# A two-layer hybrid trunk on one core: stationary weight tiles set off by 128 or 192 bytes instead of 64

## The chip, the core and the metric

The kernel runs on one core of one Trainium2 chip. The metric is the device time of one execution in microseconds (us), the median over several runs. Below, TensorE is PE and its separate row for weight loads is PEld; VectorE is DVE, ScalarE is ACT, GpSimd is POOL, and SP is the engine that issues nearly all DMAs.

## What is computed

A sequence of 256 tokens of width 2048 goes through two layers. Each layer is a token mixer and an MLP, each behind an RMSNorm whose scale and shift come from a condition vector `c`:

```python
for i in range(DEPTH):                      # DEPTH = 2
    sh1, sc1, g1, sh2, sc2, g2 = split(silu(c) @ ada_w[i] + ada_b[i])
    h = modulate(rmsnorm(x, norm_mix[i]), sh1, sc1)
    y = attn_pool_mixer(h, ...) if i % 2 == 0 else ssd_mixer(h, ...)
    x = x + g1 * y
    h = modulate(rmsnorm(x, norm_ffn[i]), sh2, sc2)
    x = x + g2 * (square(relu(h @ ffn_w1[i])) @ ffn_w2[i])   # 2048 -> 8192 -> 2048
return rmsnorm(x, final_norm)
```

Everything is float32. Layer 0 mixes by dilated window attention and pooling, layer 1 by a Mamba-2 style SSD scan. Nearly all the arithmetic is in the projections: each weight is read from HBM once, 661 MB in all with the conditioning weights.

## The kernel before

**Products in three parts.** A float32 operand is split into `hi`, its value rounded to the format of the fast matmul (float32r), and `lo`, the rest. A product is three matmuls: hi by hi, hi by lo and lo by hi. The activations `h` lie turned, with the contraction on the partitions, as tiles of 256 columns of `hi` followed by 256 columns of `lo` (`Hidden.tile`, aligned to 256 bytes).

**Two ways to multiply.** Where the weights are the stationary operand (`gemm_ws` and `up_wide`, through `mm` with `one=True`, L198 to L200), each matmul loads a 128 by 128 block of weights and streams 256 columns of activations past it; every one of the three has its own weight load. The three write one accumulator of 256 columns. Where the activations are the stationary operand (`gemm_xs`, through `xs_step`, L274 to L276), 512 columns of weights stream past.

**Who uses which.** The first projection of an MLP (`up`) has the weights stationary, the second (`down`) the activations. In the first MLP a wide sweep (`up_wide`) does the first quarter of `up` row by row with eight accumulators; in the second MLP the first block goes through `opening`, whose matmuls are 512 and 256 columns in turn (L245, L246). After that an MLP alternates: four `down` blocks of 192 matmuls of 512 columns, then three or four `up` blocks of 192 matmuls of 256 columns. The attention mixer uses `gemm_ws` for q, k and the pooling input, between the heads' small matmuls; the SSD mixer uses it for the conv inputs, two blocks of three accumulators for each of eight groups (the first of all goes through `opening`). The part of q that rides along in the attention mixer's first sweep (`half_row`) goes through the same `mm`.

**Where the weights lie.** A weight chunk of 1 MB comes in by one DMA into `raw`; `split` (L162) makes `hi` on ACT (L166) and `lo` on DVE (L167), in two halves. `hi` and `lo` are tiles of a pool with four buffers each, whose start is a multiple of `ALIGN` = 256 bytes, and the data begin `off` elements behind the start. `gemm_ws` with `one=True` and `load_row` pass `off` = `SHIFT` = 16 elements, which is 64 bytes; `gemm_xs`, `opening` and `half_row` pass nothing, so their data begin on the multiple of 256 bytes. A block of 128 columns is 512 bytes on a partition, so every stationary block of `gemm_ws` starts 64 bytes past a multiple of 256.

**What sets the order.** The code is written in the order in which each engine runs it; semaphores are set by the framework from the tiles. PE has no work of its own to choose from. Conditioning tiles (`ada_run`, L86) are fed in between by a counter (`Feed`).

Of the kernel before, what the change touches and what calls it, by code (L numbers as in the profile page):

```python
# [9 lines left out]
F32R = mybir.dt.float32r  # L10
# [5 lines left out]
P = 128  # L16
T = 256
D = 2048
# [2 lines left out]
GROUPS = 8  # L21
WINDOWS = (2, 4, 8, 16)

ALIGN, SHIFT = 256, 16


C_NMIX, C_NFFN, C_FIN, C_ADAB = 0, 32, 64, 80
# [11 lines left out]
def trunk(ctx, tc, xin, cb, fin, adaT, par, m0, m1, tri_in, icnt, pw_in,  # L39
# [5 lines left out]
    wp = ctx.enter_context(tc.tile_pool(name="weights", bufs=4))  # L45
# [3 lines left out]
    misc = ctx.enter_context(tc.tile_pool(name="miscp", bufs=3, space=PSUM))  # L49
    dram = ctx.enter_context(tc.tile_pool(name="scratch", bufs=1, space=DRAM))  # L50


    ones = const.tile([P, P], F32, name="ones")
    V.memset(ones, 1.0)
# [45 lines left out]
    def ada_jobs(l, kinds, n=4):  # L100
        jobs = []
        for k0 in range(0, KT, n):
            for kt in range(k0, k0 + n):
                for i in kinds:
                    jobs.append((l, i, kt, n if kt == k0 + n - 1 else 0))
        return jobs
# [47 lines left out]
    def load(ap, nk, width, off=0):  # L154

        raw = wp.tile([P, D], F32, name="raw")
        SP.dma_start(raw[:, 0:nk * width], ap)
        half = nk // 2
        parts = [split(wp, raw[:, s * half * width:(s + 1) * half * width], half, off) for s in range(2)]
        feed[0].tick()  # L160
        return parts

    def split(pool, src, rows, off=0):
        n = src.shape[1]
        hi, lo = (pool.tile([P, D // 2 + SHIFT], F32R, name=name, align_bytes=ALIGN)[:, off:off + n] for name in ("hi", "lo"))
        S.activation(hi, src, AF.Copy)  # L166
        V.tensor_tensor(lo, src, hi.bitcast(F32), op=ALU.subtract)  # L167
        return hi.rearrange("p (k w) -> p k w", k=rows), lo.rearrange("p (k w) -> p k w", k=rows), rows

    class Stream:  # L170
# [5 lines left out]
        def half(self, i):  # L176
            while len(self.halves) <= i:
                n = len(self.halves)
                ap, nk = self.aps[n // 2]
                if n % 2 == 0:  # L180
                    self.raw = wp.tile([P, D], F32, name="raw")
                    SP.dma_start(self.raw[:, 0:nk * self.width], ap)
                size = nk // 2 * self.width
                self.halves.append(split(wp, self.raw[:, (n % 2) * size:(n % 2 + 1) * size], nk // 2))
                if n % 2:
                    feed[0].tick()
            return self.halves[i]

    def load_row(ap, pool):

        raw = pool.tile([P, D // 2], F32, name="rawh")
        SP.dma_start(raw, ap)
        return split(wp, raw, 1, SHIFT)

    def mm(acc, hi, lo, r, first, last, one=False, skip=False):

        if one:
            PE.matmul(acc, hi, r[:, 0:T], start=first, stop=False, skip_group_check=skip)  # L198
            PE.matmul(acc, hi, r[:, T:2 * T], start=False, stop=False, skip_group_check=skip)  # L199
            PE.matmul(acc, lo, r[:, 0:T], start=False, stop=last, skip_group_check=skip)  # L200
        else:
            PE.matmul(acc, hi, r, start=first, stop=False)
            PE.matmul(acc[:, T:2 * T], lo, r[:, 0:T], start=False, stop=last)
# [47 lines left out]
    def gemm_ws(aps, rhs, width, kouter=False, one=False, before=None):  # L251

        nt = width // P
        acc = [accp.tile([P, 512], F32, name="acc") for _ in range(nt)]
        if one:
            acc = [a[:, 0:T] for a in acc]
        kt = 0
        total = sum(n for _, n in aps)
        for ap, nk in aps:
            for hi, lo, n in load(ap, nk, width, SHIFT if one else 0):  # L260
                if before:
                    before(kt)
                order = [(t, j) for j in range(n) for t in range(nt)] if kouter else [(t, j) for t in range(nt) for j in range(n)]
                for t, j in order:
                    k = kt + j
                    ts = slice(t * P, (t + 1) * P)
                    mm(acc[t], hi[:, j, ts], lo[:, j, ts], rhs(k), k == 0, k == total - 1, one)
                kt += n
        return acc
# [30 lines left out]
    def chunks(ap, n=4):  # L300
        return [(ap[c], n) for c in range(ap.shape[0])]
# [172 lines left out]
    def up_wide(h, jobs):  # L474

        for i in range(1, 4):
            h.turn_out(i, 0)
        for i in range(4):
            h.turn_out(i, 1)
        with tc.tile_pool(name="sweep1", bufs=4) as fp:  # L480
            acc = [accp.tile([P, 512], F32, name="acc") for _ in range(5)] + [misc.tile([P, 512], F32, name="mp") for _ in range(3)]
            for kt in range(KT):
                for half in range(2):
                    if half == 0:
                        h.make(kt, h.xr[:, kt, :])
                    elif jobs:
                        ada_run(jobs.pop(0))
                    hi, lo, _ = load_row(w1w[kt, :, half * 1024:(half + 1) * 1024], fp)
                    for j in range(8):
                        n = half * 8 + j  # L490
                        ts = slice(j * P, (j + 1) * P)
                        mm(acc[n // 2][:, (n % 2) * T:(n % 2 + 1) * T], hi[:, 0, ts], lo[:, 0, ts], h(kt),
                           kt == 0 and n % 2 == 0, kt == KT - 1, True, True)
        return acc

    def mlp(l, h, nx, wide=()):
# [3 lines left out]
        with tc.tile_pool(name=f"mlp{l}", bufs=2) as mp:  # L500
# [17 lines left out]
            def up(q, b, first=False):  # L518
                acc = opening(h, h.stream, 4) if first else gemm_ws(chunks(w1[l, q * 4 + b]), h, 512, one=True)
                ht = new_hid(q, b)  # L520
                for t in range(4):
                    z = new_z()
                    if first:
                        evac(acc[t], z)
                    squared_relu(z if first else acc[t], z, ht, t)
# [53 lines left out]
    def mixer0(ctx0, jobs2, following):  # L579
# [54 lines left out]
        with tc.tile_pool(name="mix0", bufs=2) as mp:  # L634
# [69 lines left out]
            for b in range(6):  # L704
                if b:
                    acc = gemm_ws(chunks(wqk[b - 1]), h, 512, one=True)
                else:
                    acc = [qacc[t // 2][:, (t % 2) * T:(t % 2 + 1) * T] for t in range(4)]
                for t in range(4):
                    q = mp.tile([P, T], F32, name="qk", bufs=9)  # L710
                    S.activation(q, acc[t], AF.Copy)
                    tiles.append(q)
                while len(tiles) >= 6:
                    six, tiles = tiles[:6], tiles[6:]
                    for par in range(2):
                        head(pair[0], par, [(six[0], six[1]), (six[2], six[3]), (six[4], six[5])])
                    pair[0] += 1
            acc = gemm_ws(chunks(wu), h, 512, one=True)
            for gi in range(4):
                u = wins[gi % 2]  # L720
# [286 lines left out]
    h = mixer0(ada_jobs(0, (G1,)) + jobs[:early], wide_input)  # L1007
    feed[0] = Feed(ada_jobs(0, (G2,)) + ada_jobs(1, (SC1, SH1)) + ada_jobs(1, (G1,)), 104)
    nx = Hidden(1, SC1, SH1, stream=Stream(chunks(sx[0, 0]), 384))
    mlp(0, h, nx, jobs[early:])  # L1010
    feed[0] = Feed(ada_jobs(1, (SC2, SH2)), 90)
    h, nx = nx, Hidden(1, SC2, SH2, stream=Stream(chunks(w1[1, 0]), 512))
    mixer1(h, nx)
    feed[0] = Feed(ada_jobs(1, (G2,)), 40)
    mlp(1, nx, Ending())


# [90 lines left out]
```

## Time and profile before

| | us |
|---|---|
| Median of 3 runs (2559.2 to 2566.05) | 2560.23 |
| The profiled execution | 2565.11 |
| Its span from the first to the last instruction | 2563.3 |
| PE busy | 2480.7 (97%) |
| Weight loads busy (PEld) | 2217.8 (87%) |
| DVE busy | 1855.4 (72%) |
| ACT busy | 1301.8 (51%) |

The profiled execution is 4.9 us above the median of the runs. PE's busy time says little by itself: matmuls are pipelined and overlap, so one that is shown as 0.28 us long is followed by the next after 0.11 to 0.12 us. The pace is read from start to start in the timeline, and a change of pace also shows in the mean duration of a group. Times below are from the start of the span. The wide sweep lies at 394 to 487, the rest of the first MLP at 487 to 1112, the SSD mixer at 1112 to 1867 and the second MLP at 1867 to 2552; the windows in the rows below follow them. The last number of a window's row is GB/s.

### The profile page before, as it was taken

The numbers are of one execution on the slowest core, as the hardware profiler recorded it, in microseconds if no ns is written. First come the engines' busy times: TensorE is split into PE (matmuls) and PEld (weight loads), VectorE is DVE, ScalarE is ACT, GpSimd is POOL, SyncE is SP. The second block draws the span as 40 slices with busy tenths as digits, with TensorE's granted clock in tenths as the row PEclk, the third lists the DMA queues.
The fourth block names the chain that finished last, engine by engine and source line by source line (L and its number), as shares of the span: only waits on it lengthen the run. The fifth ranks groups of instructions, "written<-read, shape, count | busy, mean of one in ns | idle before, by whom it ended". The sixth has DMA issues, their size and how long they took to land.

```text
span 2563.3 us, 39160 instructions
## 1 busy us (share of the span) xinstructions
PE 2480.7 (97%) x15752; PEld 2217.8 (87%) x15752; DVE 1855.4 (72%) x2432; ACT 1301.8 (51%) x1927; POOL 18.1 (1%) x76
## 2 busy tenths in 40 slices
PE   6899989999999999999999999999999999999998
PEld 5589879989889899888888878888898998998996
DVE  7977798667777886778887888776776655456555
ACT  4355546644435445457664654664554453453453
POOL 0000000000000000000000000000000000000000
PEclk9999999999999999999999999999999999999999
DMA  9988898688887887746677777655567765555553
GB/s 392 417 341 311 299 334 291 249 305 325 309 327 292 299 316 293 268 165 233 242 276 255 244 258 251 205 187 185 191 249 277 265 245 197 185 193 192 186 189 124
DMA packets 117830, 664.02 MB, mean 259 GB/s; under 512 B 11664, under 2 KB 28432, under 8 KB 49424
## 3 DMA queue, kind: packets, MB, share of 16 engines
q1 hardware_dynamic: 117440, 661.42, 71.2%
q8 instruction: 123, 2.02, 0.3%
q14 instruction: 59, 0.48, 0.1%
q10 hardware_dynamic: 208, 0.10, 0.0%
HBM read 659.28 MB, written 2.20 MB: 258 GB/s over the span
## 4 chain that ended last, share of the span: by engine, by line
PE 82%; DVE 8%; DMA 5%; ACT 2%; issue 2%; POOL 0%; SPq 0%; ACTq 0%; DVEq 0%; POOLq 0%
PE acc L275 13%; PE acc L276 13%; PE acc L274 13%; PE acc L200 12%; PE acc L198 12%; PE acc L199 12%; DMA raw<-in_adaT_dram 5%; DVE lo L167 3%; DVE raw L86 2%; PE mp L903 1%; DVE cv L837 1%; ACT hi L166 1%; PE mp L697 0%; PE mp L393 0%; PE mp L199 0%
## 5 line engine op out<-in xcount | busy, mean ns | idle before, releaser
L166 ACT ACTIVATE hi<-raw 128x1024 fp32r<-128x1024 f32 (+1 forms) x800 | 818.5, 1026 | 962.1 <-PE acc L276 539.5
L167 DVE TENSOR_TENSOR lo<-raw,hi 128x1024 fp32r<-128x1024 f32 (+1 forms) x800 | 935.6, 1179 | 490.3 <-ACT hi L166 487.6
L200 PE MATMUL acc<-h,lo 128*128 128x256 f32 x2992 | 836.4, 281 | 7.3 <-DVE lo L167 7.1
L198 PE MATMUL acc<-h,hi 128*128 128x256 f32 x2992 | 839.1, 281 | 1.4 <-DVE dt_v L783 0.8
L199 PE MATMUL acc<-h,hi 128*128 128x256 f32 x2992 | 839.3, 281 | 0.0
L199 PEld LDWEIGHTS acc<-h,hi 128*128 128x128 f32 x2992 | 569.7, 190 | 2.2 <-issue 1.7
L200 PEld LDWEIGHTS acc<-h,lo 128*128 128x128 f32 x2992 | 561.3, 188 | 10.9 <-DVE lo L167 9.2
L198 PEld LDWEIGHTS acc<-h,hi 128*128 128x128 f32 x2992 | 564.2, 189 | 6.9 <-issue 4.3
L86 DVE SCALAR_TENSOR_TENSOR raw<-raw,cond 128x2048 f32<-128x2048 f32 x192 | 439.2, 2288 | 99.7 <-DMA raw<-in_adaT_dram 99.3
L274 PE MATMUL acc<-hi,hid 128*128 128x512 f32 x1024 | 398.6, 389 | 0.0
L275 PE MATMUL acc<-lo,hid 128*128 128x512 f32 x1024 | 398.4, 389 | 0.0
L276 PE MATMUL acc<-hi,hid 128*128 128x512 f32 x1024 | 398.3, 389 | 0.0
L274 PEld LDWEIGHTS acc<-hi,hid 128*128 128x128 f32 x1024 | 192.2, 188 | 39.9
L276 PEld LDWEIGHTS acc<-hi,hid 128*128 128x128 f32 x1024 | 192.2, 188 | 39.9
L275 PEld LDWEIGHTS acc<-lo,hid 128*128 128x128 f32 x1024 | 192.2, 188 | 39.5
L275 PE MATMUL acc<-lo,h 128*128 128x512 f32 x288 | 114.4, 397 | 2.3 <-DVE lo L167 2.3
L276 PE MATMUL acc<-hi,h 128*128 128x512 f32 x288 | 116.5, 405 | 0.0
L274 PE MATMUL acc<-hi,h 128*128 128x512 f32 x288 | 113.9, 397 | 0.3 <-ACT hi L166 0.3
L166 ACT ACTIVATE hi<-rawh 128x1024 fp32r<-128x1024 f32 x64 | 60.7, 949 | 97.2 <-DMA rawh<-in_wvq_dram 60.5
L275 PE MATMUL acc<-lo,yn 128*128 128x512 f32 x224 | 87.6, 391 | 0.0
L274 PE MATMUL acc<-hi,yn 128*128 128x512 f32 x224 | 87.5, 391 | 0.0
L276 PE MATMUL acc<-hi,yn 128*128 128x512 f32 x224 | 87.4, 390 | 0.0
(230 smaller groups left out, 2342.3 us busy)
## 6 DMA issues: line engine op xcount, KB each, us to landing
raw<-in_w_dram SPq DMA_DIRECT2D x240, 1024.0 KB, 5.0
raw<-in_adaT_dram SPq DMA_DIRECT2D x192, 1024.0 KB, 6.6
raw<-in_sx_dram SPq DMA_DIRECT2D x64, 768.0 KB, 4.3
raw<-in_sz_dram SPq DMA_DIRECT2D x32, 1024.0 KB, 5.0
raw<-in_swo_dram SPq DMA_DIRECT2D x32, 1024.0 KB, 4.9
raw<-in_wqk_dram SPq DMA_DIRECT2D x20, 1024.0 KB, 6.9
rawh<-in_wvq_dram SPq DMA_DIRECT2D x32, 512.0 KB, 12.2
rawh<-in_w1w_dram SPq DMA_DIRECT2D x32, 512.0 KB, 6.3
```

Source lines behind the costliest of these rows:

```text
L86: V.scalar_tensor_tensor(raw, raw, 1.0, cond, op0=ALU.mult, op1=ALU.mult, accum_out=acc_ada[l][:, i * KT + kt:i * KT + kt + 1])
L166: S.activation(hi, src, AF.Copy)
L167: V.tensor_tensor(lo, src, hi.bitcast(F32), op=ALU.subtract)
L198: PE.matmul(acc, hi, r[:, 0:T], start=first, stop=False, skip_group_check=skip)
L199: PE.matmul(acc, hi, r[:, T:2 * T], start=False, stop=False, skip_group_check=skip)
L200: PE.matmul(acc, lo, r[:, 0:T], start=False, stop=last, skip_group_check=skip)
L274: PE.matmul(acc[c], ah, hi, start=first, stop=False)
L275: PE.matmul(acc[c], ah, lo, start=False, stop=False)
L276: PE.matmul(acc[c], al, hi, start=False, stop=last)
L837: V.scalar_tensor_tensor(cv, xp[:, j:j + T], pcol(C_CW + j * 48 + ch), cv, op0=ALU.mult, op1=ALU.add)
L903: PE.matmul(ps[:, i * 64:(i + 1) * 64], em[c][:, i, :], xdt[c][:, i * 64:(i + 1) * 64], start=True, stop=True)
```

## The change

The constant `SHIFT` becomes a list with one number that is set anew while the program is written: 48 elements (192 bytes) for the attention mixer, 32 (128 bytes) for the first MLP with its wide sweep and for the SSD mixer, and 48 again for the second MLP. The tiles grow from 1024 + 16 to 1024 + 48 elements, to hold the larger offset.

```diff
-ALIGN, SHIFT = 256, 16
+ALIGN, ROOM = 256, 48
+SHIFT = [48]
...
-        hi, lo = (pool.tile([P, D // 2 + SHIFT], F32R, name=name, align_bytes=ALIGN)[:, off:off + n] for name in ("hi", "lo"))
+        hi, lo = (pool.tile([P, D // 2 + ROOM], F32R, name=name, align_bytes=ALIGN)[:, off:off + n] for name in ("hi", "lo"))
...
-        return split(wp, raw, 1, SHIFT)
+        return split(wp, raw, 1, SHIFT[0])
...
-            for hi, lo, n in load(ap, nk, width, SHIFT if one else 0):
+            for hi, lo, n in load(ap, nk, width, SHIFT[0] if one else 0):
...
     nx = Hidden(1, SC1, SH1, stream=Stream(chunks(sx[0, 0]), 384))
+    SHIFT[0] = 32
     mlp(0, h, nx, jobs[early:])
...
     mixer1(h, nx)
     feed[0] = Feed(ada_jobs(1, (G2,)), 40)
+    SHIFT[0] = 48
     mlp(1, nx, Ending())
```

The order of the instructions on every engine is the same in both programs, row for row, and only line numbers differ (L198 to L200 become L201 to L203). With the alignment of 256 bytes, a tile of 4160 bytes and one of 4288 both take 4352, and in the two built programs no tile lies at another address. What differs is where the data begin in `hi` and `lo`: of the 9264 matmuls with a set-off stationary block, 5232 have 128 instead of 64 bytes and 4032 have 192; the 192 of `half_row` stay at 0.

## Rows read from the trace of the kernel before

**Rows 1.** Page, part 1: busy us (share of the span) and instructions.

```profile
PE 2480.7 (97%) x15752; PEld 2217.8 (87%) x15752; DVE 1855.4 (72%) x2432; ACT 1301.8 (51%) x1927; POOL 18.1 (1%) x76
```

**Rows 2.** Page, part 4: shares of the chain that ended last, by engine.

```profile
PE 82%; DVE 8%; DMA 5%; ACT 2%; issue 2%; POOL 0%; SPq 0%; ACTq 0%; DVEq 0%; POOLq 0%
```

**Rows 3.** Windows: length, busy (count) PE, PEld, DVE, ACT, POOL, clock, DMA.

```profile
487.00:1112.00 625.00, 621.68 (x3854) 560.33 (x3852) 460.79 (x488) 302.22 (x433) 0.69 (x3) 1.00 0.80 294
1112.00:1867.00 755.00, 734.17 (x4575) 647.62 (x4576) 609.46 (x958) 426.55 (x642) 12.78 (x57) 0.99 0.66 226
1867.00:2552.00 685.00, 684.74 (x4414) 624.83 (x4414) 387.91 (x403) 327.24 (x465) 0.55 (x1) 1.00 0.59 210
```

**Rows 4.** Windows, L199's matmuls alone: length, PE busy (count), clock, DMA.

```profile
394.00:487.00 93.00, 72.55 (x259) 0.99 0.77 275
487.00:1112.00 625.00, 214.59 (x765) 1.00 0.80 294
1112.00:1867.00 755.00, 201.42 (x720) 0.99 0.66 226
1867.00:2552.00 685.00, 269.08 (x960) 1.00 0.59 210
```

**Rows 5.** Timeline of PE, first MLP: start us, duration, instruction.

```profile
1000.04 0.28 PE L199 MATMUL acc<-h,hi 128*128 128x256 f32 x1
...
1003.93 0.28 PE L199 MATMUL acc<-h,hi 128*128 128x256 f32 x1
```

**Rows 6.** Timeline of PE, SSD mixer.

```profile
1275.84 0.28 PE L199 MATMUL acc<-h,hi 128*128 128x256 f32 x1
...
1278.90 0.28 PE L199 MATMUL acc<-h,hi 128*128 128x256 f32 x1
```

**Rows 7.** Groups from 1000 to 1012: count, busy us, mean ns, idle before.

```profile
L199 PE MATMUL acc<-h,hi 128*128 128x256 f32 x34 | 9.6, 281 | 0.0
L199 PEld LDWEIGHTS acc<-h,hi 128*128 128x128 f32 x35 | 6.7, 192 | 0.0
```

**Rows 8.** Groups by line from 1276 to 1282.

```profile
L199 PE MATMUL acc<-h,hi 128*128 128x256 f32 x19 | 5.2, 276 | 0.0
L199 PEld LDWEIGHTS acc<-h,hi 128*128 128x128 f32 x18 | 3.4, 188 | 0.0
```

**Rows 9.** Timeline of PE, second MLP, from `down` to `up`.

```profile
2375.83 0.39 PE L276 MATMUL acc<-hi,hid 128*128 128x512 f32 x1
2376.06 0.28 PE L198 MATMUL acc<-h,hi 128*128 128x256 f32 x1
...
2377.47 0.28 PE L198 MATMUL acc<-h,hi 128*128 128x256 f32 x1
```

**Rows 10.** Timeline of PE, SSD mixer, from `opening` to `gemm_ws`.

```profile
1140.73 0.28 PE L198 MATMUL acc<-h,hi 128*128 128x256 f32 x1
...
1142.21 0.28 PE L199 MATMUL acc<-h,hi 128*128 128x256 f32 x1
```

**Rows 11.** Timeline of PE, attention mixer's first sweep, weights at offset 0.

```profile
44.61 0.28 PE L199 MATMUL mp<-h,hi 128*128 128x256 f32 x1
...
45.44 0.28 PE L200 MATMUL mp<-h,lo 128*128 128x256 f32 x1
...
45.92 0.40 PE L616 MATMUL acc<-hi,h 128*128 128x512 f32 x1
```

**Rows 12.** Timeline of PE, attention mixer, `gemm_ws` behind a head's float32 matmuls.

```profile
261.89 0.39 PE L198 MATMUL acc<-h,hi 128*128 128x256 f32 x1
...
262.92 0.28 PE L200 MATMUL acc<-h,lo 128*128 128x256 f32 x1
...
263.60 0.28 PE L200 MATMUL acc<-h,lo 128*128 128x256 f32 x1
```

**Rows 13.** Groups, DVE: 850 to 940 (mostly `down`); 940 to 1035 (`up`).

```profile
L167 DVE TENSOR_TENSOR lo<-raw,hi 128x1024 fp32r<-128x1024 f32 x34 | 41.0, 1220 | 13.5 <-ACT hi L166 13.5
...
L167 DVE TENSOR_TENSOR lo<-raw,hi 128x1024 fp32r<-128x1024 f32 x34 | 41.0, 1222 | 13.9 <-ACT hi L166 13.9
```

More of the change, by code (lines that the diff above doesn't have):

```diff
@@ L1014, in trunk @@
     feed[0] = Feed(ada_jobs(1, (G2,)), 40)
+    SHIFT[0] = 48
     mlp(1, nx, Ending())
```

## The prediction

> **What bounds the kernel now.** I read the page's busy times and chain first, then windows by stage, then the timeline of PE from start to start. The reader should see that PE sets the time: it is busy 2480.7 us, 97% of the span [rows 1] and makes 82% of the chain that ended last [rows 2]. In the two MLPs it never rests: 621.68 of 625 us and 684.74 of 685 us, with DVE at 460.79 and 387.91 us and DMA at 0.80 and 0.59 [rows 3]. In the SSD mixer it leaves some 21 us of 755 [rows 3]. So in the MLPs a matmul that starts earlier moves the end by as much.
>
> The change touches nothing but where a stationary block begins, so the question is the pace of L198 to L200. The timeline shows two paces for the same instruction at the same offset of 64 bytes. In the first MLP 33 matmuls take 1003.93 - 1000.04 = 3.89 us, 117.9 ns each [rows 5]; in the SSD mixer 27 take 3.06 us, 113.3 ns each [rows 6]. I call them the slow and the fast rhythm. The groups show them too: 281 ns a matmul in the slow one, and one weight load of the three lengthened to 192 ns [rows 7], against 276 and 188 ns [rows 8]. Nobody waits for another engine in either (idle 0.0), and the granted clock is 1.00, the 2.4 GHz level, so the difference of some 4.5 ns lies between weight load and stream inside PE.
>
> A rhythm, once begun, holds until PE is held up. Which one begins depends on what stood ahead. After a `down` block it is the slow one: 12 matmuls in 2377.47 - 2376.06 = 1.41 us, 117.5 ns each [rows 9]. All six such places in the MLPs look like this. After `opening` it is the fast one: 13 in 1142.21 - 1140.73 = 1.48 us, 113.8 ns, the first few included [rows 10].
>
> A third rhythm is seen at offset 0, in the attention mixer's first sweep: 11 matmuls in 1.31 us, 119.1 ns each, the last four of them 120 ns [rows 11]. All 16 sweeps repeat it. The matmuls ahead of it are plain float32 ones; at offset 64 a block that begins behind such matmuls of a head, at 261.89, goes in the fast rhythm a microsecond later, 6 matmuls in 0.68 us [rows 12]. So the offset does move the pace, by up to 6.7 ns of 113, and 0 is the bad end of what the trace shows. It does not show 128 or 192.
>
> **The change part by part.** First what costs nothing. Instructions, order and tile addresses are the same. ACT and DVE write `hi` and `lo` at the new offset: `lo` takes 1220 ns in a stretch mostly at offset 0 and 1222 ns in one mostly at 64 [rows 13], so the writers do not feel it. If they did, the MLPs' cover is wide (DVE leaves 164 of 625 us [rows 3]).
>
> Then the pace. A triple (L198 to L200) takes 3 x 117.8 = 353.3 ns slow and 3 x 113.3 = 340.0 ns fast, a difference of 13.3 ns. How many triples are slow I read from L199's mean, between 276 (all fast) and 281 (all slow):
> - wide sweep: 72.55 / 259 = 280.1 ns [rows 4]; the timeline shows nothing but the slow rhythm, so 259 x 13.3 = 3.4 us.
> - rest of the first MLP: 214.59 / 765 = 280.5 ns [rows 4], nine tenths slow: 0.9 x 765 x 13.3 = 9.2 us.
> - second MLP: 269.08 / 960 = 280.3 ns [rows 4], 0.86 slow: 0.86 x 960 x 13.3 = 11.0 us.
> - SSD mixer: 201.42 / 720 = 279.75 ns [rows 4], which waits lengthen too, so at most three quarters slow: 7.2 us at most. The timeline gives about six in ten, 5.7 us.
> - attention mixer: 384 triples by the code, about a quarter slow, 1.2 us.
>
> So the MLPs hold 23.6 us of slow rhythm and the mixers up to 7. The other way, 0.1 x 765 + 0.14 x 960 fast triples in the MLPs and about 290 in each mixer could turn slow: (211 + 580) x 13.3 ns = 10.5 us. And if all 3088 set-off triples went at the 120 ns of offset 0, that would be 360 - 340 = 20 ns more than fast and 6.7 ns more than slow: about 2300 triples of the slow rhythm x 6.7 + 790 of the fast x 20 = 15.4 + 15.8 = 31 us. These are the bounds: 31 us gained, 31 us lost.
>
> Which value? The trace shows that 64 bytes away from the bad offset the fast rhythm exists but is not found after `down`. Both new offsets lie away from 0 in the cycle of 256 bytes to which the tiles are aligned: 128 is the farthest and 192 as far as 64, on the other side. I take it that the fast rhythm is easier to find there, and that it holds through the long `up` blocks, since nothing disturbs them. For the MLPs I take the whole 23.6 us. In the mixers most blocks are short, begin behind small matmuls and have waits that swallow part of a gain, so I take nothing there. The sum is 2565.1 - 23.6 = 2541.5 us for the profiled execution, and 4.9 less against the median of the runs: 2536.6, say **2537 us**.
>
> **A rule that speaks against it.** The rows show a pace that differs by offset and by what stood ahead [rows 5, 6, 11]. The Trainium skill ("TensorE: Matmul & The Clock Gate", section "Step-by-step: what each phase is for") says that PE has two independent read ports, one for the stream and one for weight loads, so that loading the next weights takes no bandwidth from the running matmul. By that rule the address of the weights could not matter and the time would be 2560 us. The rows agree with it only in the fast rhythm, and speak against it at 117.8 and 120 ns.
>
> **The rivals.**
> - *Half of it.* One of the two offsets finds the fast rhythm after `down` and the other does not, or only the wide sweep changes. First MLP alone: 2560.2 - 12.6 = 2548 us; second alone: 2549.
> - *The same rhythms.* The offset within the 256 bytes decides nothing; what stands ahead of a block decides alone, as rows 9 and 10 suggest by themselves, since there the offset is the same and the pace differs. Then 2560 us, give or take the 4 us by which the mixers shift. For it: both rhythms are seen at one offset. Against it: the 120 ns at offset 0.
> - *Fast blocks turn slow*, mostly in the mixers, while the MLPs stay as they are: up to 10.5 us, 2571 us. It decides where more than 8 us, three quarters of the fast triples, go over.
> - *The rhythm of offset 0 at 128 bytes.* If what counts is whether load and stream reach the same spot of a repeating pattern together, a half cycle may be as bad as none, and the 5232 matmuls of the first MLP and the SSD mixer go at 120 ns. About 1380 triples of the slow rhythm x 6.7 + 365 of the fast x 20 = 9.2 + 7.3 = 16.5 us, 2577 us; with the second MLP and the attention mixer too, 2591. It decides from the first `up` block of the first MLP on, and nothing hides it, because PE never rests there.
> - *The change does not do what it says* is excluded, as the built program has the offsets where the text puts them.
>
> **How the numbers follow.** Fast rhythm in both MLPs, 2528 to 2543: 0.40. Half of it, 2543 to 2553: 0.15. The same, 2553 to 2568: 0.25. Fast turned slow, about 2570: 0.06. The rhythm of offset 0, 2572 to 2592: 0.14. A measurement tells about 0.3% from no change, some 8 us; so faster 0.55, same 0.25, slower 0.20. The low end of the range is all fast, mixers too: 2560 - 31 = 2529, rounded to 2528. The high end is 2572, which leaves out the 120 ns case, 0.14, and little else.
>
> **What would show it.** Right: L201 to L203 at 276 ns in the MLPs instead of 281, starts 113.3 ns apart from the first few matmuls after `down`, and no 192 ns load. Half: one MLP at 276 and the other at 281. Same: 281 in both. The bad rival: starts 120 ns apart and a mean above 281 in the wide sweep. The pace of `down` and the durations of L166 and L167 should not change in any case. The prediction is wrong if the fast rhythm does not begin after a `down` block; it would be wrong in its ground if the rhythms were fast there and the time still did not move, which would mean that PE is not what the MLPs wait for.

## The result and the profile after

| | before | after |
|---|---|---|
| Median of the runs (us) | 2563.11 (2559.2 to 2566.05, 4 runs) | 2577.64 (2576.95 to 2578.63, 4 runs) |
| Profiled execution | 2565.11, span 2563.3 | 2578.33, span 2576.5 |

The ratio is 1.0058, with an interval of 1.0040 to 1.0076: the changed kernel is slower, by some 14 us. The ratios here and below are estimated from all the runs of a comparison, and need not equal the quotient of the two medians. The prediction was 2537 us with a range of 2528 to 2572. The time lies outside it, and the sign is the other one.

The page of the changed kernel answers to [rows 1, 2]: busy times, then the shares of the chain that ended last.

```profile
PE 2498.2 (97%) x15752; PEld 2234.7 (87%) x15752; DVE 1856.5 (72%) x2432; ACT 1305.0 (51%) x1927; POOL 18.2 (1%) x76
...
PE 84%; DVE 6%; DMA 5%; ACT 2%; issue 2%; POOL 0%; SPq 0%; ACTq 0%; POOLq 0%; DVEq 0%
```

DVE and ACT work as long as before (1.1 and 3.2 us more), PE and its loads 17.5 and 16.9 us longer, with the same instructions. The windows by stage answer to [rows 3]; the columns are the same.

```profile
491.00:1121.00 630.00, 628.47 (x3869) 567.07 (x3867) 462.43 (x490) 304.47 (x437) 0.69 (x3) 1.00 0.79 293
1121.00:1879.00 758.00, 740.00 (x4577) 653.24 (x4578) 610.10 (x958) 428.35 (x644) 12.79 (x57) 0.99 0.65 226
1879.00:2565.00 686.00, 685.86 (x4410) 626.14 (x4410) 387.21 (x401) 327.41 (x464) 0.55 (x1) 1.00 0.59 210
```

PE never rests in the MLPs, as before, and the granted clock is 1.00 there in both kernels. So nobody waits longer; the matmuls follow one another more slowly. The timeline of PE shows it. First the entry from `down` into `up` in the first MLP, where the offset is now 128 bytes (start us, duration, instruction; L201 to L203 are the three of the prediction):

```profile
602.60 0.40 PE L279 MATMUL acc<-hi,hid 128*128 128x512 f32 x1
602.83 0.29 PE L201 MATMUL acc<-h,hi 128*128 128x256 f32 x1
...
604.39 0.28 PE L202 MATMUL acc<-h,hi 128*128 128x256 f32 x1
```

13 matmuls take 604.39 - 602.83 = 1.56 us, 120.0 ns each, where before 12 behind a `down` block took 117.5 ns each [rows 9]. The same in the SSD mixer behind `opening`:

```profile
1149.71 0.28 PE L201 MATMUL acc<-h,hi 128*128 128x256 f32 x1
...
1151.49 0.28 PE L201 MATMUL acc<-h,hi 128*128 128x256 f32 x1
```

15 in 1.78 us, 118.7 ns, against 113.8 ns [rows 10]. So 128 bytes has two rhythms as well, and a block can change over. In the first MLP a small matmul of the conditioning (L124) comes between two rows of a block:

```profile
628.04 0.28 PE L201 MATMUL acc<-h,hi 128*128 128x256 f32 x1
...
631.28 0.28 PE L201 MATMUL acc<-h,hi 128*128 128x256 f32 x1
...
631.64 0.27 PE L124 MATMUL mp<-ident,mod 128*16 128x128 f32 x1
...
632.46 0.28 PE L201 MATMUL acc<-h,hi 128*128 128x256 f32 x1
...
635.31 0.28 PE L201 MATMUL acc<-h,hi 128*128 128x256 f32 x1
```

Ahead of it 27 matmuls take 3.24 us, 120.0 ns each; behind it 24 take 2.85 us, 118.75 ns each. All six places behind `down` in this kernel's first and second MLP begin in the slower rhythm of their offset, 120.0 ns at 128 bytes and 117.8 at 192, as those of the kernel before begin at 117.8 at 64. And in the second MLP, where it is 192 bytes:

```profile
2390.03 0.28 PE L201 MATMUL acc<-h,hi 128*128 128x256 f32 x1
...
2391.09 0.28 PE L201 MATMUL acc<-h,hi 128*128 128x256 f32 x1
```

9 in 1.06 us, 117.8 ns: exactly the slow rhythm [rows 5]. The mean durations that I had named as the mark are less sharp. These are the groups from 770 to 800 (first MLP, 128 bytes), and from 2400 to 2430 (second MLP, 192 bytes):

```profile
L203 PE MATMUL acc<-h,lo 128*128 128x256 f32 x85 | 24.2, 285 | 0.0
L202 PE MATMUL acc<-h,hi 128*128 128x256 f32 x84 | 23.9, 284 | 0.0
L201 PE MATMUL acc<-h,hi 128*128 128x256 f32 x84 | 23.6, 281 | 0.0
```

```profile
L203 PE MATMUL acc<-h,lo 128*128 128x256 f32 x86 | 24.1, 280 | 0.0
L201 PE MATMUL acc<-h,hi 128*128 128x256 f32 x86 | 24.0, 279 | 0.0
L202 PE MATMUL acc<-h,hi 128*128 128x256 f32 x85 | 23.7, 279 | 0.0
```

The second group shows 279 ns at a pace of 117.8, where [rows 7] show 281 ns at the same pace. A duration in this row is modelled, so I take the pace from start to start from here on. The table gives its mean over the pairs of neighbouring set-off matmuls of a stage whose starts lie at most 130 ns apart; wider gaps are waits and are summed apart, as what they hold beyond 117 ns. The number behind a stage counts its neighbouring pairs, those with a wider gap too (in the wide sweep its matmuls).

| stage (pairs) | ns before | ns after (offset) | pairs x difference, us | wider gaps, us | stage length, us |
|---|---|---|---|---|---|
| attention mixer (1112) | 114.38 | 117.78 (192) | +3.8 | 4.8 -> 5.1 | +4.6 up to here |
| wide sweep (768) | 117.79 | 118.67 (128) | +0.7 | 0.4 -> 0.9 | |
| rest of first MLP (2299) | 117.53 | 119.70 (128) | +5.0 | 2.9 -> 1.5 | 745.7 -> 750.1 |
| SSD mixer (2125) | 116.10 | 119.05 (128) | +6.3 | 7.5 -> 6.3 | 726.6 -> 729.3 |
| second MLP (2875) | 117.15 | 117.78 (192) | +1.8 | 0.6 -> 0.5 | 696.0 -> 697.6 |

The paces lose 17.6 us. The span grew by 13.2 us: in the SSD mixer 2.7 of 6.3 us come out at the end, and its wider gaps shrink from 7.5 to 6.3 us, so waits took up a part. At neither new offset did a single block go at 113.3 ns.

### The profile page after: what moved, and what is told of

Its sections match the earlier page's. It is cut to its first block, busy times and chain, and to the rows that moved or that the text cites. A ratio compares the mean times of both kernels' runs of the same rounds, so it can differ in the third digit from the quotient of the medians.

```text
span 2576.5 us, 39160 instructions
## 1 busy us (share of the span) xinstructions
PE 2498.2 (97%) x15752; PEld 2234.7 (87%) x15752; DVE 1856.5 (72%) x2432; ACT 1305.0 (51%) x1927; POOL 18.2 (1%) x76
## 4 chain that ended last, share of the span: by engine, by line
PE 84%; DVE 6%; DMA 5%; ACT 2%; issue 2%; POOL 0%; SPq 0%; ACTq 0%; POOLq 0%; DVEq 0%
PE acc L279 13%; PE acc L277 13%; PE acc L278 13%; PE acc L203 13%; PE acc L202 13%; PE acc L201 12%; DMA raw<-in_adaT_dram 4%; DVE lo L170 2%; DVE raw L89 2%; PE mp L906 1%; ACT hi L169 1%; DVE cv L840 1%; PE mp L700 0%; PE mp L202 0%; PE mp L201 0%
## 5 line engine op out<-in xcount | busy, mean ns | idle before, releaser
L170 DVE TENSOR_TENSOR lo<-raw,hi 128x1024 fp32r<-128x1024 f32 (+1 forms) x800 | 937.5, 1179 | 532.1 <-ACT hi L169 530.4
L203 PE MATMUL acc<-h,lo 128*128 128x256 f32 x2992 | 841.9, 283 | 3.4 <-DVE lo L170 3.2
L202 PE MATMUL acc<-h,hi 128*128 128x256 f32 x2992 | 843.2, 282 | 0.0
L201 PE MATMUL acc<-h,hi 128*128 128x256 f32 x2992 | 841.1, 282 | 1.2 <-DVE dt_v L786 0.7
L201 PEld LDWEIGHTS acc<-h,hi 128*128 128x128 f32 x2992 | 564.4, 189 | 7.1 <-issue 4.2
L203 PEld LDWEIGHTS acc<-h,lo 128*128 128x128 f32 x2992 | 562.3, 188 | 6.8 <-DVE lo L170 5.0
L202 PEld LDWEIGHTS acc<-h,hi 128*128 128x128 f32 x2992 | 563.7, 188 | 2.2 <-issue 1.7
L278 PE MATMUL acc<-lo,h 128*128 128x512 f32 x288 | 114.8, 399 | 3.3 <-DVE lo L170 3.3
```

Source lines behind the costliest of these rows:

```text
L278: PE.matmul(acc[c], ah, lo, start=False, stop=False)
```

## The experiments

The theories at the outset were these. A: each offset has rhythms of its own. B, the rival *the same rhythms*: what stands ahead of a block decides, and the offset is only a bystander. Later ones took up what makes the two rhythms at 64 bytes. The diffs are against the changed kernel where nothing else is said.

**One offset everywhere: 0, and 192.**

```diff
-    SHIFT[0] = 48
+    SHIFT[0] = 0
...
-    SHIFT[0] = 32
+    SHIFT[0] = 0
```

> All weights at 0 bytes. Theory 'offset decides': 119 to 120 ns in all stages, as the attention mixer's first sweep shows at 0; 9264 matmuls at about 119.3 instead of the mean of about 116.8 of the kernel before, some 20 us more than before less what waits swallow, 2578 to 2583 us. Rival 'what stands ahead decides': fast rhythm of 113.3 behind the opening blocks, 117.8 behind the down blocks, and the time of before, 2563 us.

Measured: 2588.11 us against 2563.9, ratio 1.0097 (1.0082 to 1.0112), some 5 us above the expected range. Every stage goes at 120 ns (119.8 to 120.0 in the table's measure). Two rows of its timeline in the second MLP, with 9 matmuls in 1.08 us:

```profile
2400.03 0.28 PE L202 MATMUL acc<-h,hi 128*128 128x256 f32 x1
...
2401.11 0.28 PE L202 MATMUL acc<-h,hi 128*128 128x256 f32 x1
```

The second MLP loses (120.0 - 117.15) x 2875 = 8.2 us by pace, and lasts 704.9 instead of 696.0. So the offset alone moves the time by 24 us, and a lost nanosecond in the second MLP is paid in full.

```diff
-    SHIFT[0] = 32
+    SHIFT[0] = 48
```

> All set-off weights at 192 bytes, in the first MLP and the SSD mixer too. Theory 'offset decides' (each offset within 256 bytes has rhythms of its own): 117.8 ns from start to start in all stages, as the changed kernel shows it in the attention mixer and the second MLP, no 119 or 120 ns in the first MLP and no 113.3 anywhere; then the first MLP gives back about 5 us and the SSD mixer some 3 us of the changed kernel's loss, time near 2570 us. Rival 'the larger tile or something besides the offset': the first MLP stays near 119.7 ns and the time near 2578 us.

Measured: 2573.74 us (2567.74 to 2579.55), ratio 1.0047 (1.0030 to 1.0064). The pace is 117.78 in both mixers and in the second MLP. The wide sweep of the profiled execution is the exception, with 114.04, and part of the block behind it: so 192 can go in the fast rhythm too, and did so in no other stage. The runs spread over 12 us, of which this sweep explains (117.78 - 114.04) x 768 = 2.9; the rest is open.

**Every 16 bytes.** Each `up` block of the two MLPs gets an offset of its own, the other stages 64 bytes.

```diff
+OFFS = {(0, 1, 0): 16, (0, 1, 1): 4, (0, 1, 2): 36, (0, 1, 3): 52, (0, 2, 0): 8, (0, 2, 1): 40, ...}
...
+                SHIFT[0] = OFFS.get((l, q, b), 16)
```

> Every up block of the MLPs that gemm_ws makes has its own offset, multiples of 16 bytes from 0 to 240 (first after a down block: 16, 32, 48, 80, 96, 112); the mixers and the wide sweep are at 64. Theory 'the whole 64-byte line counts': 16, 32 and 48 go like 0 (119 to 120 ns), 80, 96 and 112 like 64 (113.3 or 117.8), 144 and 160 like 128 (119 to 120), 208 to 240 like 192 (117.8). Theory 'the finer place counts': offsets off the 64-byte grid show rhythms of their own, slower than 120 where a block crosses one line more, or the fast one after a down block. Theory 'what stands ahead decides': 117.8 in all blocks behind down whatever the offset.

Measured, as the pace in the blocks (one execution, 2567.46 us; 27 blocks of 192 matmuls, most offsets in two of them):

| offset, bytes | 0 | 16 | 32 | 48 | 64 | 80 | 96 | 112 |
|---|---|---|---|---|---|---|---|---|
| ns | 120.0 | 118.3 | 118.3 | 117.8 / 118.3 | 113.3 / 117.8 | 118.7 | 117.3 | 120.0 |

| offset, bytes | 128 | 144 | 160 | 176 | 192 | 208 | 224 | 240 |
|---|---|---|---|---|---|---|---|---|
| ns | 118.6 | 120.0 | 120.0 | 118.1 | 117.8 | 116.7 | 116.7 | 120.0 |

The theory of the whole 64-byte line falls, since 16 to 48 bytes do not go like 0, nor 112 like 64. Of the finer place it holds that offsets between have paces of their own, but none is above 120.0 and none goes fast behind `down`. Theory B falls: behind `down`, 80 bytes goes at 118.7, 96 at 117.3 and 112 at 120.0. It was not wholly empty either. The block at 64 bytes that begins behind one at 240 goes in the fast rhythm at once, with no wait and no other matmul in between. The two blocks meet at about 1000.5 us; here are 26 matmuls at 240 in 3.12 us (120.0 ns) and 27 at 64 in 3.06 us (113.3 ns):

```profile
997.00 0.28 PE L203 MATMUL acc<-h,hi 128*128 128x256 f32 x1
...
1000.12 0.28 PE L202 MATMUL acc<-h,hi 128*128 128x256 f32 x1
...
1000.84 0.28 PE L202 MATMUL acc<-h,hi 128*128 128x256 f32 x1
...
1003.90 0.28 PE L202 MATMUL acc<-h,hi 128*128 128x256 f32 x1
```

**Whose offset? The weights' or their distance from the stream's.** In the first run `h` begins 64 bytes past a multiple of 256 as the weights do; in the second `h` at 64, the weights at 128. (A second buffer of a small tile, `cv`, goes to make room.)

```diff
-                self.h[i] = const.tile([P, 4, 2 * T], F32R, ...)
+                self.h[i] = const.tile([P, 8 * T + HOFF], F32R, ...)[:, HOFF:].rearrange("p (k w) -> p k w", k=4)
...
-                cv = mp.tile([P, T], F32, name="cv")
+                cv = mp.tile([P, T], F32, name="cv", bufs=1)
```

> The activations h, which stream past the weights, begin 64 bytes past a multiple of 256 as well, and the weights are at 64. (To make room, one conv tile of the SSD mixer has one buffer instead of two.) Theory 'relative': what counts is the weights' place against the stream's; both at 64 is like both at 0, so 119 to 120 ns in the MLPs and no 113.3. Theory 'absolute': only the weights' own place counts; 117.8 behind down blocks and 113.3 behind the opening, as in the kernel before.

Measured: 2588.66 us, and 120.0 ns in the stages that had gone at 113.3 and 117.8 at the same 64 bytes. In its first MLP (L202 to L204 are the three) 10 matmuls take 1.20 us:

```profile
769.84 0.28 PE L202 MATMUL acc<-h,hi 128*128 128x256 f32 x1
...
771.04 0.28 PE L203 MATMUL acc<-h,hi 128*128 128x256 f32 x1
```

The part that rides in the attention mixer's first sweep stayed at offset 0 with `h` at 64, which is a distance of -64 or 192: its pace went from 118.9 to 117.5, near the 117.8 of 192.

> Activations 64 bytes past a multiple of 256, weights 128 past. Theory 'relative': 64 bytes apart as in the kernel before, so 113.3 ns behind the opening and 117.8 behind the down blocks, and no 120; the time is near before, 2560 to 2568 us. Theory 'absolute': the weights are at 128, so 118.7 to 120 ns in the first MLP as in the changed kernel, and near 2585 us.

Measured: 2566.58 us beside 2567.21 of before, one execution. No block at 120; behind `down` in the first MLP, where the changed kernel went at 120.0 with the same 128 bytes, 12 matmuls take 1.42 us, 118.3 ns, and the block settles at 117.8:

```profile
597.62 0.28 PE L202 MATMUL acc<-h,hi 128*128 128x256 f32 x1
...
599.04 0.28 PE L202 MATMUL acc<-h,hi 128*128 128x256 f32 x1
```

Away from waits every longer stretch of set-off matmuls in this run settles at 113.3 or 117.8 ns, the two rhythms of 64, so the smaller `cv` is not what slowed the run before. In these two runs, one execution each, what counts is the distance of the stationary block from the streamed one, and not where either lies. That it goes by 256 bytes rests on the -64 that goes like 192; distances beyond were not tried one by one.

**The two halves of the change apart.**

```diff
-    SHIFT[0] = 48
+    SHIFT[0] = 16
...
     SHIFT[0] = 32
...
-    SHIFT[0] = 48
+    SHIFT[0] = 16
```

> Only the part with 128 bytes (first MLP and SSD mixer), 64 elsewhere. Theory 'each offset has its own rhythms': from the paces of the two traces, wide sweep 768 matmuls x (118.67 - 117.79) = 0.7 us, rest of the first MLP 2299 x (119.70 - 117.53) = 5.0, SSD mixer 2125 x (119.05 - 116.10) = 6.3: 12 us over before at most, 9 to 12 as waits of the SSD mixer swallow some. Rival 'the loss lies in one stage that the traces do not split': nearly all 14 us or nearly none.

Measured, 128 bytes in the first MLP and the SSD mixer alone: 2576.74 us against 2567.21, ratio 1.0032 (1.0009 to 1.0056). Paces 118.6 in the wide sweep, 118.7 and 120.0 in the rest, 119.3 in the SSD mixer. The first MLP lasts 751.8 us, the SSD mixer 731.6.

```diff
-    SHIFT[0] = 32
+    SHIFT[0] = 16
```

> Only the part with 192 bytes (attention mixer and second MLP), 64 elsewhere. Theory 'each offset has its own rhythms': attention mixer 1112 x (117.78 - 114.38) = 3.8 us, second MLP 2875 x (117.78 - 117.15) = 1.8 us: 3 to 6 us over before. Rival as in the run with 128 alone: 14 us or none.

Measured, 192 bytes in the attention mixer and the second MLP alone: 2570.35 us, ratio 1.0023 (1.0006 to 1.0039). Both go at 117.5 to 117.8. The two ratios less 1 add up to 0.0055, beside 0.0058 of the whole; by medians they are 9.5 and 3.1 us, so the split is good to a few us only. In this execution the wide sweep, at 64 bytes, went at 114.35 instead of 117.79: the same block at the same offset finds one rhythm in one execution and the other in the next. The first MLP was none the shorter for it: 748.4 us, where the kernel before took 745.7.

**Choosing the entry.** If a block at 64 bytes keeps the rhythm in which it starts, the matmuls ahead of it can be chosen. The first 24 matmuls of each `gemm_ws` block, half a chunk, get an offset of their own: 0 in the mixers and the first MLP, 240 in the second.

```diff
-    def load(ap, nk, width, off=0):
+    def load(ap, nk, width, off=0, lead=None):
...
-        parts = [split(wp, raw[:, s * half * width:(s + 1) * half * width], half, off) for s in range(2)]
+        parts = [split(wp, raw[:, s * half * width:(s + 1) * half * width], half, off if s or lead is None else lead) for s in range(2)]
```

> Weights at 64 bytes, but the first half chunk of each gemm_ws block (24 matmuls of 192) begins at another offset: 0 in the mixers, the wide sweep's first row and the first MLP, 240 in the second MLP. Theory 'the rhythm at 64 is chosen by how a block is entered': coming out of the 120 ns rhythm, where each weight load ends late, the rest of a block goes at 113.3 ns, as behind the opening and as one block of the sweep did (offset 240 ahead, then 64). All blocks fast: about 30 us less, of which 26 x 24 x 6.7 ns = 4 us are paid for the lead; 2535 to 2545 us. Theory 'what decides is the run of 512-column matmuls ahead, or chance': the rest of a block goes at 117.8 as before, and the time is 2563 to 2568 us.

Measured: 2560.37 us against 2567.21, ratio 0.9975 (0.9962 to 0.9988), faster than the kernel before. The timeline behind `down`, first with the lead at 0 (L203 to L205 are the three):

```profile
755.27 0.28 PE L203 MATMUL acc<-h,hi 128*128 128x256 f32 x1
...
758.14 0.28 PE L203 MATMUL acc<-h,hi 128*128 128x256 f32 x1
...
761.91 0.28 PE L205 MATMUL acc<-h,lo 128*128 128x256 f32 x1
```

24 in 2.87 us (119.6 ns), then 32 at 64 bytes in 3.77 us, 117.8 ns: the slow rhythm. The expectation that a lead at 0 would open the fast one was wrong, and with it the 2535 to 2545 us; in the first MLP only a few blocks turn fast later on, behind an interruption. And with the lead at 240, in the second MLP:

```profile
2200.02 0.28 PE L203 MATMUL acc<-h,hi 128*128 128x256 f32 x1
...
2202.83 0.28 PE L203 MATMUL acc<-h,hi 128*128 128x256 f32 x1
...
2204.55 0.28 PE L203 MATMUL acc<-h,hi 128*128 128x256 f32 x1
...
2205.91 0.28 PE L203 MATMUL acc<-h,hi 128*128 128x256 f32 x1
```

24 in 2.81 us (117.1 ns), and later in the block 12 in 1.36 us, 113.3 ns. All 15 `up` blocks of `gemm_ws` in the second MLP do so, with a mean of 113.9 over whole blocks, lead included. By pace that is (117.15 - 113.86) x 2875 = 9.5 us; the stage went from 696.0 to 687.3 us. The whole gained 6.8 us by medians, less than this one stage.

**The lead at 240 everywhere.** In the wide sweep it is the first half of every fourth row. The diff is against the kernel with the lead at 0 and 240.

```diff
-    LEAD[0] = 0
+    LEAD[0] = 60
```

> Weights at 64 bytes, the first half chunk of every gemm_ws block at 240, and in the wide sweep the first half of every fourth row. Theory 'the rhythm at 64 is chosen by how a block is entered, and 240 ahead enters the fast one': 113.9 ns mean in every up block of both MLPs as in the second MLP of the run before; first MLP 2299 x (117.53 - 113.87) = 8.4 us, wide sweep 768 x (117.79 - 114) = 2.9, second MLP 2875 x (117.15 - 113.87) = 9.4, SSD mixer up to 4.5 where its blocks are not disturbed: 21 to 25 us less than before. Rival 'the second MLP is fast for another reason (its place, its h)': the first MLP stays at 117.8 or mixed, and the gain is about 9 us.

Measured: 2556.46 us against 2563.22, ratio 0.9967 (0.9954 to 0.9979), the lowest median of all, but a gain of 6.8 us and not the 21 to 25 expected. The paces are 113.9 in the wide sweep, 114.5 in the rest of the first MLP, 114.8 in the SSD mixer and 113.9 in the second MLP. But the first MLP, which by pace should be 3.0 + 7.0 = 10.0 us shorter, went only from 745.7 to 743.7. The wider gaps say where some of it went: 2.2 instead of 0.4 us in the wide sweep and 6.7 instead of 2.9 in the rest. Behind a wait a block at 64 bytes can also fall back to 117.8, so that the rest has a mean of 114.5 and not 113.9. PE's waits in the first MLP, and DVE's, suggest the cause (times in us: total, count, longest), first in the kernel before, then here:

```profile
PE acc L200 <- DVE lo L167: 2.3, 2, 1.3
DVE raw L86 <- DMA raw<-in_adaT_dram: 67.8, 44, 3.9
```

```profile
PE acc L205 <- DVE lo L172: 6.3, 7, 1.6
DVE raw L91 <- DMA raw<-in_adaT_dram: 122.1, 59, 6.8
```

DVE waits for the conditioning weights, and the `lo` of the next block comes behind them. DVE's total alone proves little: it was 113.4 us with 128 bytes alone, at 119.7 ns, and 111.2 with the lead at 0, at 117.4. The windows of before and of this kernel over the same stretch:

```profile
520.00:1090.00 570.00, 570.00 (x3531) 514.59 (x3530) 422.46 (x434) 265.63 (x359) 0.00 (x0) 1.00 0.82 304
```

```profile
520.00:1090.00 570.00, 565.78 (x3531) 507.28 (x3530) 419.91 (x436) 265.65 (x360) 0.00 (x0) 1.00 0.82 304
```

PE does the same 3531 matmuls in both and now rests for 4.2 us; the traffic is the same 304 GB/s. In this stretch PE's faster pace buys nothing, as if the transfers now set it; the last two runs test that. The chain of this kernel reads alike, with DMA at 12% where it was 5% [rows 2]:

```profile
PE 71%; DMA 12%; DVE 9%; issue 4%; ACT 3%; POOL 0%; SPq 0%; DVEq 0%; ACTq 0%; POOLq 0%
```

**One steady offset, 208 bytes.** Its pace does not hang on the entry, so it tests the pace map without any rhythm to find.

```diff
-    SHIFT[0] = 48
+    SHIFT[0] = 52
...
-    SHIFT[0] = 32
+    SHIFT[0] = 52
```

> All set-off weights at 208 bytes. The sweep showed 116.67 ns in each of two blocks at 208. Theory 'each offset has its own rhythms': 116.7 in all stages, no 113.3 and no 117.8; against the mean of 116.8 of before no measurable change of time, within 3 us. Theory 'the sweep's rhythms came from the offset of the block ahead': 208 shows other paces here, 113 to 120.

Measured: 2566.63 us, ratio 1.0006 (0.9992 to 1.0019); 116.7 ns in every block of every stage, whatever stood ahead. The kernel before, weighted by the pairs of the table, has a mean of 116.7 too, and the time is the same within the noise: equal sums of paces give equal times, without a change of rhythm.

**Taking transfers out of the first MLP.** To see whether the loads are what holds the lead's gain back there, 16 conditioning tiles (`G1` of layer 1) move to the SSD mixer; once with the lead at 240 everywhere, once in the kernel before; the diff is against these two.

```diff
-    feed[0] = Feed(ada_jobs(0, (G2,)) + ada_jobs(1, (SC1, SH1)) + ada_jobs(1, (G1,)), 104)
+    feed[0] = Feed(ada_jobs(0, (G2,)) + ada_jobs(1, (SC1, SH1)), 104)
...
-    feed[0] = Feed(ada_jobs(1, (SC2, SH2)), 90)
+    feed[0] = Feed(ada_jobs(1, (G1,)) + ada_jobs(1, (SC2, SH2)), 90)
```

> The lead of 240 bytes in every block, and 16 of the conditioning tiles (1 MB each) that the first MLP's counter feeds are fed in the SSD mixer instead, ahead of that stage's own. Theory 'the first MLP's gain was swallowed by the conditioning loads' (there DVE waits 122 us for them with the lead, 68 us before, at the same 295 GB/s): the first MLP, 743.7 us long with the lead, comes down by some 7 to 9 us, the SSD mixer grows by a few at most, and the time is 3 to 9 us under that of the lead alone. Rival 'something else in the first MLP holds it': its length stays within 2 us of 743.7 and the time is that of the lead alone or more, as the SSD mixer has 37 us of DVE work more.

> The kernel before (64 bytes, no lead) with the same 16 conditioning tiles fed in the SSD mixer. Theory 'swallowed by the conditioning loads': in the kernel before PE never rests in the first MLP, so that its length stays at 744 to 746 us and the time does not fall, within 4 us of before; what the move gives appears only together with the lead. Rival 'the move itself is the gain': it falls by as much as the run with both does against the lead alone.

Measured with the lead: 2559.36 us against 2566.55, ratio 0.9972 (0.9958 to 0.9986). In the first MLP DVE's wait is down to 33.4 us and PE does 37 matmuls more in the same stretch without a rest:

```profile
DVE raw L91 <- DMA raw<-in_adaT_dram: 33.4, 27, 3.6
```

```profile
520.00:1090.00 570.00, 570.00 (x3568) 513.33 (x3567) 395.37 (x406) 269.11 (x363) 0.00 (x0) 1.00 0.76 278
```

Yet the stage lasts 743.5 us, no less than with the lead alone, and the whole gains no more: the expected 7 to 9 us off the stage and 3 to 9 us off the time did not come. Ahead of the first run of `down` blocks there is a wait that was not there:

```profile
PE acc L203 <- ACT hi L171: 5.6, 1, 5.6
```

Without the lead the same move costs: 2575.95 us, ratio 1.0036 (1.0023 to 1.0049), with the same wait of 5.6 us, and a first MLP of 752.7 us; the expectation of no more than 4 us was missed. What the lead gives is seen where the wait lies behind: from the first `up` matmul behind `down` to the last `up` matmul of the stage, 2880 matmuls later. These are the two ends with the lead alone, then with the lead and the move:

```profile
595.94 0.28 PE L203 MATMUL acc<-h,hi 128*128 128x256 f32 x1
...
1018.96 0.28 PE L205 MATMUL acc<-h,lo 128*128 128x256 f32 x1
```

```profile
601.25 0.28 PE L203 MATMUL acc<-h,hi 128*128 128x256 f32 x1
...
1015.86 0.28 PE L205 MATMUL acc<-h,lo 128*128 128x256 f32 x1
```

| these 2880 matmuls, us | 64 bytes alone | lead at 240 |
|---|---|---|
| conditioning tiles where they were | 422.9 | 423.0 |
| 16 of them moved | 422.9 | 414.6 |

The lead gives nothing in this part of the stage, the move gives nothing, and the two together give 8.3 us. So the transfers had held the lead's gain back there, as far as one execution of each can show. The move costs 6.9 us of the first MLP without the lead: 4.6 ahead of these matmuls, where the wait lies, and 2.3 behind them. Why it costs them is open.

## Why the prediction was wrong

**What held.** PE bounds the kernel, the two rhythms exist, nobody's wait explains them, and the offset moves the pace. A rhythm does hold until PE is held up: in the trace of the kernel before, none of the 47 undisturbed stretches of more than 36 set-off matmuls changes its pace. In its first MLP a stretch at 117.8 ns ends in a wait for `lo`, and the stretch behind it goes at 113.4:

```profile
491.63 0.28 PE L199 MATMUL acc<-h,hi 128*128 128x256 f32 x1
493.18 0.38 PE L200 MATMUL acc<-h,lo 128*128 128x256 f32 x1 [1.27 <-DVE lo L167]
```

The writers did not feel the new offsets: `lo` took 1179 ns in the mean of either page (L167 before, L170 after). A nanosecond in the second MLP is paid in full (8.7 of 9.5 us with the lead, and 0 bytes cost 8.9 for 8.2).

**The step that failed** is the choice of value: "that the fast rhythm is easier to find there". I argued from the distance to the one bad offset, 0, as if the pace got better the farther one went. It does not: 128 bytes goes at 118.7 to 120.0 ns and 192 at 117.8, and the 23.6 us for the MLPs became a loss of 7.5 by pace. The fast rhythm was seen at 64 bytes, and at 192 in one sweep of one execution and the block behind it; the other fourteen offsets, most of them tried in one or two blocks, never showed it. And behind `down` blocks at 64, 128 and 192 bytes all began in the slower of their two rhythms: what stands ahead chose the slow one at each. One row at offset 0 and two at 64 could not tell a slope from a map with many values, and I should have left the sign to the bounds.

**The rivals.** *The rhythm of offset 0 at 128 bytes* had 0.14, and was what happened in the first MLP and the SSD mixer: it gave 16.5 us; the paces lost 0.7 + 5.0 + 6.3 = 12.0 us, and the half of the change with 128 bytes alone measured 0.32%, some 8 us. The size is smaller since 128 has a rhythm of 118.7 beside the one of 120.0, and the wide sweep and much of the SSD mixer go in it. *Fast blocks turn slow* happened as well, in the other half: 192 holds the slow rhythm everywhere, 3.8 us in the attention mixer and 1.8 in the second MLP by pace, 0.23%, some 6 us, when measured alone (3.1 us by medians). I had treated the two as alternatives. They lie in different stages and add up, to 2577.6. That this is so near the 2577 of the first rival is chance.

**The bounds.** The upper price was 120 ns for all set-off matmuls, 31 us. Measured with offset 0 everywhere: 0.97%, some 25 us, at just that pace. The lower one, 31 us gained, was not reached: with the lead the paces were near 114 and the kernel gained 0.33%, some 8 us. The ground of it, that the MLPs never rest and so pay in full, failed in the first MLP, where PE at 113.9 and 114.5 outran the conditioning weights. A busy share of 621.68 of 625 us [rows 3] says that PE is the bound now; how far ahead of the next bound it may get, DVE's 67.8 us of waits for those weights in the same stage could have warned me.

**The rule that I weighed.** The traces differ from it: the address of the stationary block relative to the stream's moved the matmul by up to 6.7 ns of 113.3, at 1.00 of the granted clock and with no wait. The Trainium skill ("TensorE: Matmul & The Clock Gate", section "Step-by-step: what each phase is for") has two independent read ports and no loss of bandwidth to the running matmul. By that rule all the kernels in which nothing but offsets differ would have come out at the time of before; they lie between 2556 and 2588 us. The measurement decides. What inside PE or the memory ties the two reads together, no run here shows.

**The mark.** 276 against 281 ns, by which I wanted to tell the cases apart, would have misled: 192 bytes shows 279 at the pace at which 64 bytes showed 281.

## What to carry to other kernels

Where TensorE loads a new stationary block for every short stream and never waits, take its pace from start to start, and treat the distance of the two operands in SBUF, modulo 256 bytes, as a parameter to be measured in steps of 16 bytes; here no offset could be inferred from its neighbour (116.7 ns at 224 bytes, 120.0 at 240). An offset with two paces is worth looking into, since a few matmuls at another offset ahead of a block can set the better one. Before a gain of pace is credited to a stage, look at who waits for transfers there, since that stream becomes the bound next.

## What the hardware showed that I had not expected

- The pace of load and stream takes several values between 113.3 and 120.0 ns that go by the distance of the two operands, with a jump from 116.7 at 224 bytes to 120.0 at 240. At the 2.4 GHz level (granted clock 1.00) the ends are 272 and 288 periods for 256 columns, 16 and 32 more than the columns.
- Some distances have two rhythms: 113.3 and 117.8 ns at 64 and 192 bytes, 118.7 and 120.0 at 128. A block keeps the one that it has until a wait or another matmul interrupts it, and then it may change. At 64 bytes 24 matmuls at 240 ahead lead into 113.3, 24 at 0 into 117.8.
- The rhythm of one and the same block differs between executions (wide sweep at 64 bytes: 117.79 and 114.35 ns, 2.6 us by pace), and runs of the kernel before lay between 2557.8 and 2573.9 us in one comparison. How much of that spread is rhythm is open.
